# Hymba decoder step: product with v by a difference of blocks, softmax division on ScalarE, last weights split once, the second sample task later

## The chip, the cores and the metric

The program runs on one core of one Trainium2 chip. The metric is the device time of one execution in microseconds (us); the median of three runs of the kernel before is 1681.65 us (1681.14 to 1681.77). One of its executions was also profiled. PE is TensorE (PEld its weight loads), DVE is VectorE, ACT is ScalarE, POOL is GpSimd, SP is SyncE, which issues all transfers here.

## The reference

One layer of a decoder with two heads side by side, in fp32, for 512 prompt tokens and 8 x 8 sampled tokens (576 columns, T) at width 2048:

```python
h = rmsnorm(x, norm_pre); u = h @ w_in          # 2048 x 9760, split into q k v g_a z xbc dt
o_a = swa_prompt(q, k, v, sink)                 # window 128, blocks of 128: each block sees itself and the one before
# sampled tokens: swa_step against a cache of 128 keys
attn_out = rmsnorm(o_a * silu(g_a), attn_norm)
xs, B, C = silu(causal_conv(xbc)); y, h_new = ssd(xs, dt, A, B, C, h0, 128)
ssm_out = grouped_rmsnorm((y + D * xs) * silu(z), ssm_norm)
out = concat(attn_out, ssm_out) @ w_out         # 4096 x 2048
return x + rmsnorm(out, norm_post), new k, v, conv and ssm states
```

## The kernel before

Features lie on partitions, tokens on columns, in two halves p of 288 columns (H). Each weight block (128 x 128) is split in two fp32r parts, high (a ScalarE cast, L332) and low (a VectorE subtraction, L335); so is each block of activations (XU). A product of one weight block with one half is three matmuls of 288 columns, mm3 (L351 to L353). 3352 of them are the bulk of the program: first the columns of w_in (blocks of B, C, x, z, then k, v, and 16 pairs q, g for the attention), then w_out in two passes over the ssm half (pass 0) and the attention half (pass 1). Most blocks from the attention on are computed in pairs, by seven products in place of eight; those use sums of weights made on GpSimd (L269).

Each weight unit of 128 x 512 is loaded into one of nine tiles `raw`, split into one of four tiles `w` (`split_next`, three units ahead of PE), and its `raw` is then free for a later load.

All else is written as Python generators. A scheduler counts a tick for each mm3; `yield n` lets n ticks of mm3 be issued before the generator goes on. The order of instructions on every engine is thereby fixed when the program is built; on the chip each engine works through its own order and waits on semaphores. A generator that goes on later in ticks stands later in every engine's order and in SP's queue.

Names that the change and the prediction touch:

- `rms_x` sums the squares of x (VectorE adds, L564), reduces them on PE (L463) and spreads 1/rms as tile R (L497, copy L613), with which every output of w_in is multiplied (L446, L1206).
- `dt_task` makes the step sizes and decays of the ssm heads: a chain of small VectorE operations (L752 to L773) on a bias loaded from `dtb`, then small matmuls (L782 on).
- Per group g of 8 ssm heads: `scan_task` for four chunks and, as c = 4, the sampled tokens (`sample`, eight `seq` per group: ScalarE L1373, matmul L1378, VectorE L1381); then `gate_task`, whose `renorm` (L1133) reads each block back from memory (`m_d`), scales it and stores it.
- `qb_task`, two per head pair, 32 in all, is the attention: scores (L955, L956), maximum, exponentials (ScalarE L992), denominator (L995, L996), division (L997), transposes on PE (L1002), masks (L1010, L1012), product with v (L1022).
- `smp_task`, one per group of eight pairs (pr = 0, 1), is the attention of the sampled tokens (scores L1063, L1064; L1070 to L1098). The second one runs where the attention ends and pass 0 begins. `attn_end` waits for it, and then takes the norm over the attention (L463 at 1307 us) and runs `renorm` over 16 blocks, which pass 1 reads.
- `mix_task(h)` loads the normed blocks and splits them (L540, L545) as XU for pass h.
- In the last pass blocks 14 and 15 are computed for half p = 0 and then for p = 1, so that `end_task(0)`, the final norm of the first half, lies beside the matmuls of the second: `inv_rms` (L463), spread (L497), then per block a multiplication by 1/rms (L1650), an addition of the residual x (L1654) and a store. The weights of those two blocks are split anew for each half. `x_task` loads the residual.

Of the kernel before, what the change touches and what calls it, by code (L numbers as in the profile page):

```python
# [9 lines left out]
F32 = mybir.dt.float32  # L10
# [168 lines left out]
def kern(ctx: ExitStack, tc: tile.TileContext, a: dict, o: dict):  # L179
# [121 lines left out]
    for p in range(2):  # L301
        for u in range(8):
            jobs.append([b + u, [], [b + u] if p else []])
# [293 lines left out]
    def rms_x():  # L597
# [6 lines left out]
        yield 8  # L604
# [126 lines left out]
    def dt_task():  # L731
# [3 lines left out]
        yield 32  # L735
# [158 lines left out]
    def v_task(st, vn):  # L894
# [10 lines left out]
        S.copy(st.vt[:, :512], pa)  # L905
        V.tensor_copy(vts[:TS, st.pr], pb[:TS, :P])
# [31 lines left out]
    def qb_task(st, jj, m, u):  # L938
# [58 lines left out]
        V.tensor_tensor(p4, p4, den.unsqueeze(2).broadcast_to([P, 4, P]), ALU.mult)  # L997
        tiny.put(t1, t2)
        yield 11
# [8 lines left out]
        for w, tr in enumerate((stri, tri)):  # L1008
            if f and w == 0:
                V.tensor_tensor(pT4[0][:, :, 1], ptv[:, :, 1], tr.unsqueeze(1).broadcast_to([P, 2, P]), ALU.mult)  # L1010
            else:
                V.tensor_tensor(pT[w][:, :512].rearrange("p (e k) -> p e k", e=4), pt.rearrange("p (e k) -> p e k", e=4),  # L1012
                                tr.unsqueeze(1).broadcast_to([P, 4, P]), ALU.mult)
        banks.put(pt)
        yield 9
        for q in range(2):
            qb = 2 * m + q
            w0 = 0 if qb else 1
            for w in range(w0, 2):
                for hf in range(2):  # L1020
                    kc = 128 * (qb - 1 + w) + 64 * hf
                    PE.matmul(u.po[64 * hf:64 * hf + 64, 128 * qb:128 * qb + 128], st.vt[:, kc:kc + 64], pT4[w][:, hf, q],  # L1022
                              start=w == w0, stop=w == 1)
# [3 lines left out]
    def o_task(st, jj, u):  # L1027
# [8 lines left out]
        if st.npv == 8:  # L1036
            smalls.put(st.vt)
# [6 lines left out]
    def smp_task(st):  # L1044
# [9 lines left out]
        yield from wait(lambda: len(st.q) == 8 and st.kready and st.vready)  # L1054
        osb = yield from banks.get()
# [278 lines left out]
    def sample(grp, n, cs, C, Bt, xes, sms, E):  # L1334
# [34 lines left out]
        def seq(b, h0):  # L1369
# [6 lines left out]
            yield 10  # L1376
# [12 lines left out]
        for w in range(2):  # L1389
# [9 lines left out]
            for b, h0 in enumerate(hs, 4 * w):  # L1399
                sch.spawn(seq(b, h0))  # L1400
                yield 5
# [168 lines left out]
    split_in = [0]  # L1570

# [4 lines left out]
    def out_pass(h, evac):  # L1576
        sch.spawn(sums_task(h))
        for kind, *cs in OUT[h]:
# [11 lines left out]
            if h and cs[-1] == 7:  # L1590
                sch.spawn(x_task(0))
# [7 lines left out]
    RO = R  # L1599
# [32 lines left out]
    def end_task(p):  # L1632
# [8 lines left out]
        r = RO[:, t0:t0 + H]  # L1641
        S.copy(r, pa[:, :H])
        engine = [G if (q * NPOOL) % KB < NPOOL else V for q in range(KB)]
        for e0 in range(0, KB, 2):
# [3 lines left out]
            for c in (e0, e0 + 1):  # L1648
                v = part[c][:, t0:t0 + H]
                engine[c].tensor_tensor(v, v, r if engine[c] is G or e0 > 4 else pa[:, :H], ALU.mult)  # L1650
            if e0 == 4:
                banks.put(pa)
            for c in (e0, e0 + 1):
# [126 lines left out]
```

## Time and profile before

| what | value |
|---|---|
| median of three runs | 1681.65 us |
| profiled execution, its own time | 1680.61 us |
| its span, first to last instruction | 1678.8 us |
| mean granted TensorE clock | 0.981 |
| busy: PE / PEld | 1602.4 us (95%) / 1539.9 us (92%) |
| busy: DVE / ACT / POOL | 1141.9 (68%) / 718.8 (43%) / 393.6 us (23%) |
| instructions: PE / DVE / ACT / POOL | 12158 / 2247 / 1699 / 428 |

PE is busy nearly all the time, so time can only come from what PE does, from the stretches in which it waits, and from the two ends of the program. The granted clock stands at half (1.2 in place of 2.4 GHz) in a few short stretches; its mean over a stretch is the column PEclk of the table of stretches.

### The profile page before, as it was taken

The page shows a single profiled execution, that of the slowest core. Times are in us where ns is not written, and L with a number is a line of the kernel's source. Part 1 is how long each engine was busy: PE and PEld are TensorE (multiplying, and loading weights), DVE is VectorE, ACT ScalarE, POOL GpSimd, SP SyncE. Part 2 cuts the span into 40 slices and gives each one's busy share as a digit, 9 for nine tenths or more (in the row PEclk, how much of TensorE's full clock was granted, in tenths as well). Part 3 has the DMA queues.
Part 4 walks back from the last instruction along what each step waited for, and adds up shares of the span by engine and source line. Part 5 has one row for each costly group of instructions (what it writes and reads, how often), then busy time and mean ns, then how long its engine had stood idle before and what let it go on. Part 6 is the DMA issues. An engine that isn't in the chain of part 4 may idle for free.

```text
span 1678.8 us, 31783 instructions
## 1 busy us (share of the span) xinstructions
PE 1602.4 (95%) x12158; PEld 1539.9 (92%) x12158; DVE 1141.9 (68%) x2247; ACT 718.8 (43%) x1699; POOL 393.6 (23%) x428
## 2 busy tenths in 40 slices
PE   8989999999989998999999999999889999999993
PEld 8989999899989997999999999999879999999993
DVE  7656755675568556578898878888775454655557
ACT  6434434444444444444444434444544322544441
POOL 3001223112313222313222122232102211023315
PEclk9989999999999999999999999999999999999996
DMA  6334356656465547652223223233532665623333
GB/s 234 81 79 108 92 182 182 148 161 185 145 144 183 157 127 269 199 120 79 93 76 120 71 83 98 63 100 96 173 111 76 159 201 161 223 77 125 101 116 113
DMA packets 157976, 222.97 MB, mean 133 GB/s; under 512 B 32160, under 2 KB 66080, under 8 KB 157792
## 3 DMA queue, kind: packets, MB, share of 16 engines
q1 hardware_dynamic: 157824, 220.95, 44.3%
q8 instruction: 95, 1.56, 0.4%
q14 instruction: 57, 0.47, 0.1%
HBM read 182.26 MB, written 40.60 MB: 133 GB/s over the span
## 4 chain that ended last, share of the span: by engine, by line
PE 64%; DMA 9%; DVE 6%; issue 2%; ACT 1%; SPq 1%; POOL 0%; DVEq 0%; ACTq 0%
PE bank L351 19%; PE bank L353 18%; PE bank L352 18%; DMA s<-m_d 5%; DMA r_d<-t 2%; PE bank L1022 2%; DVE s L1133 1%; DVE w L335 1%; PE bank L1002 1%; PE bank L955 1%; PE bank L956 1%; DVE s L1650 1%; PE bank L1282 1%; DVE x L545 1%; PE bank L1292 1%
## 5 line engine op out<-in xcount | busy, mean ns | idle before, releaser
L351 PE MATMUL bank<-x,w 128*128 128x288 f32 x3352 | 1017.2, 303 | 6.2 <-DVE eT L423 4.1
L353 PE MATMUL bank<-x,w 128*128 128x288 f32 x3352 | 1000.6, 299 | 15.9 <-DVE w L335 15.7
L352 PE MATMUL bank<-x,w 128*128 128x288 f32 x3352 | 997.5, 298 | 2.0 <-DVE x L545 2.0
L351 PEld LDWEIGHTS bank<-x,w 128*128 128x128 f32 x3352 | 635.2, 189 | 26.6 <-issue 18.6
L353 PEld LDWEIGHTS bank<-x,w 128*128 128x128 f32 x3352 | 636.0, 190 | 20.6 <-DVE w L335 20.6
L352 PEld LDWEIGHTS bank<-x,w 128*128 128x128 f32 x3352 | 635.5, 190 | 8.0 <-issue 4.1
L335 DVE TENSOR_TENSOR w<-raw,w 128x512 fp32r<-128x512 f32 x492 | 396.8, 811 | 164.2 <-ACT w L332 155.8
L332 ACT CAST w<-raw 128x512 fp32r<-128x512 f32 x492 | 299.3, 615 | 348.0 <-PE bank L352 259.5
L269 POOL TENSOR_TENSOR raw<-raw,raw 128x512 f32<-128x512 f32 x52 | 77.1, 1483 | 188.4 <-issue 171.5
L269 POOL TENSOR_TENSOR raw<-sum,raw 128x512 f32<-128x512 f32 x26 | 33.5, 1288 | 187.9 <-DVE w L335 187.9
L1162 DVE SCALAR_TENSOR_TENSOR u<-u,c_convwb,u 128x600 f32<-128x600 f32 x72 | 63.9, 892 | 16.1 <-ACT u L1159 15.0
L992 ACT ACTIVATE m<-m,t 128x128 f32<-128x128 f32 x128 | 49.9, 391 | 33.0 <-DVE t L987 33.0
L1232 ACT ACTIVATE m<-m,a_tok 128x128 f32<-128x128 f32 (+1 forms) x160 | 52.8, 381 | 19.6 <-DMA m<-aT_d 19.6
L833 POOL TENSOR_TENSOR s<-s,s 128x512 f32<-128x512 f32 (+2 forms) x42 | 43.8, 1042 | 67.7 <-ACT s L831 66.8
L545 DVE TENSOR_TENSOR x<-s,x 128x288 fp32r<-128x288 f32 x112 | 49.1, 484 | 15.5 <-ACT x L540 15.4
L1612 POOL TENSOR_TENSOR s<-s,s 128x288 f32<-128x288 f32 x28 | 22.8, 820 | 151.4 <-ACT s L1609 151.4
L269 POOL TENSOR_TENSOR sum<-raw,raw 128x512 f32<-128x512 f32 x26 | 36.0, 1386 | 93.1 <-DMA raw<-in_win_dram 52.0
L1375 POOL TENSOR_TENSOR m<-m,dch 128x512 f32<-128x512 f32 x32 | 37.8, 1210 | 79.3 <-PE bank L1397 60.3
L1268 POOL TENSOR_TENSOR m<-m,de 128x512 f32<-128x512 f32 (+1 forms) x20 | 27.0, 1348 | 109.0 <-DVE m L1261 87.6
L1430 POOL TENSOR_TENSOR s<-s,s 128x576 f32<-128x576 f32 x16 | 24.1, 1503 | 115.4 <-DMA s<-z_d 102.5
L540 ACT CAST x<-s 128x288 fp32r<-128x288 f32 x112 | 42.5, 429 | 18.1 <-DVE s L642 12.4
L831 ACT ACTIVATE s<-s 128x512 f32<-128x512 f32 (+1 forms) x27 | 17.7, 656 | 72.2 <-POOL s L1430 44.6
(248 smaller groups left out, 1671.3 us busy)
## 6 DMA issues: line engine op xcount, KB each, us to landing
raw<-in_win_dram SPq DMA_DIRECT2D x304, 256.0 KB
raw<-in_wout_dram SPq DMA_DIRECT2D x128, 256.0 KB
s<-m_d SPq DMA_DIRECT2D x80, 288.0 KB
m_d<-s SPq DMA_DIRECT2D x48, 288.0 KB
s<-in_xT_dram SPq DMA_DIRECT2D x40, 288.0 KB
m<-aT_d SPq DMA_DIRECT2D x32, 256.0 KB
m<-in_h0T_dram SPq DMA_DIRECT2D x32, 256.0 KB
out_ss_dram<-m SPq DMA_DIRECT2D x32, 256.0 KB
```

What stands on the lines that cost most here:

```text
L269: G.tensor_tensor(dst, x, y, op)
L332: S.copy(w[:, 0], x)
L335: V.tensor_tensor(w[:, 1], x, w[:, 0].bitcast(F32), ALU.subtract)
L351: PE.matmul(out, w[:, 0, c], x[:, 0], start=start, stop=False, skip_group_check=True)
L352: PE.matmul(out, w[:, 0, c], x[:, 1], start=False, stop=False, skip_group_check=True)
L353: PE.matmul(out, w[:, 1, c], x[:, 0], start=False, stop=stop, skip_group_check=True)
L540: S.copy(t[:, 0], src)
L545: V.tensor_tensor(t[:, 1], src, t[:, 0].bitcast(F32), ALU.subtract)
L833: G.tensor_tensor(self.acc[:, c0:c0 + n], self.acc[:, c0:c0 + n], sq[:, :n], ALU.add)
L992: S.activation(p4[:, e], p4[:, e], AF.Exp, bias=nm[:, e:e + 1], scale=0.125, accum_out=den[:, e:e + 1])
L1162: V.scalar_tensor_tensor(y[:, :600], U[:, w:w + 600], cw[:, k, w:w + 1], y[:, :600], op0=ALU.mult, op1=ALU.add)
L1232: S.activation(Mv[q][:n, h, :n], Mv[q][:n, h, :n], AF.Relu, bias=a_tok[:n, c, k:k + 1], scale=-1.0)
```

## The change

- **Product with v.** With P the softmax after its transposition, and masks stri (key later than query in the block before) and tri (not later), the product was (stri P) v_before + (tri P) v_own. Since stri + tri = 1, it is (stri P)(v_before - v_own) + P v_own: `v_task` makes the difference once per group (`st.vd`), and the second mask's multiplication on VectorE (L1012 with tri) becomes a copy on ScalarE.
- **Division.** One VectorE multiplication of 128 x 512 by 1/den becomes four ScalarE activations of 128 x 128 with a scale per partition.
- **Last two blocks.** Their eight weight units leave the list of jobs; `last_units` splits them once into 16 kept tiles. `x_task(0)` starts after that, `x_task(1)` after the first half.
- **end_task.** All 16 multiplications are on VectorE and read 1/rms from the bank; the 16 additions alternate by pairs of blocks between GpSimd and VectorE, two pairs behind. The copy to R goes.
- **Ticks.** rms_x 8 to 14, dt_task 32 to 46, seq 10 to 13 with 7 in place of 5 between them, smp_task of pr = 1 waits 75 more.

```diff
@@ -298,9 +298,6 @@
     nunit[0] += 8
-    for p in range(2):
-        for u in range(8):
-            jobs.append([b + u, [], [b + u] if p else []])
@@ -601,7 +598,7 @@
         slots.put(*xr[1:])
-        yield 8
+        yield 14
         r = yield from inv_rms([xr[0]], D)
@@ -732,7 +729,7 @@
         V.tensor_tensor(dtr[:64, :T], dtr[:64, :T], R[:64], ALU.mult)
-        yield 32
+        yield 46
         An = dtb[:, 32:64]
@@ -903,6 +900,8 @@
         S.copy(st.vt[:, :512], pa)
+        st.vd = yield from smalls.get()
+        V.tensor_tensor(st.vd[:, P:512], st.vt[:, 0:512 - P], st.vt[:, P:512], ALU.subtract)
         V.tensor_copy(vts[:TS, st.pr], pb[:TS, :P])
@@ -994,9 +993,11 @@
         V.reciprocal(den, den)
-        V.tensor_tensor(p4, p4, den.unsqueeze(2).broadcast_to([P, 4, P]), ALU.mult)
+        yield 2
+        for e in range(4):
+            S.activation(p4[:, e], p4[:, e], AF.Copy, scale=den[:, e:e + 1])
         tiny.put(t1, t2)
-        yield 11
+        yield 10
         pt = yield from banks.get()
@@ -1005,12 +1006,13 @@
         pT4 = [t[:, :512].rearrange("p (f q k) -> p f q k", f=2, q=2) for t in pT]
-        for w, tr in enumerate((stri, tri)):
-            if f and w == 0:
-                V.tensor_tensor(pT4[0][:, :, 1], ptv[:, :, 1], tr.unsqueeze(1).broadcast_to([P, 2, P]), ALU.mult)
-            else:
-                V.tensor_tensor(pT[w][:, :512].rearrange("p (e k) -> p e k", e=4), pt.rearrange("p (e k) -> p e k", e=4),
-                                tr.unsqueeze(1).broadcast_to([P, 4, P]), ALU.mult)
+        S.copy(pT[1][:, :512], pt)
+        if f:
+            V.tensor_tensor(pT4[0][:, :, 1], ptv[:, :, 1], stri.unsqueeze(1).broadcast_to([P, 2, P]), ALU.mult)
+        else:
+            V.tensor_tensor(pT[0][:, :512].rearrange("p (e k) -> p e k", e=4), pt.rearrange("p (e k) -> p e k", e=4),
+                            stri.unsqueeze(1).broadcast_to([P, 4, P]), ALU.mult)
         banks.put(pt)
@@ -1018,8 +1020,8 @@
                 for hf in range(2):
-                    kc = 128 * (qb - 1 + w) + 64 * hf
-                    PE.matmul(u.po[64 * hf:64 * hf + 64, 128 * qb:128 * qb + 128], st.vt[:, kc:kc + 64], pT4[w][:, hf, q],
+                    kc = 128 * qb + 64 * hf
+                    PE.matmul(u.po[64 * hf:64 * hf + 64, 128 * qb:128 * qb + 128], (st.vd, st.vt)[w][:, kc:kc + 64], pT4[w][:, hf, q],
                               start=w == w0, stop=w == 1)
@@ -1034,7 +1036,7 @@
         if st.npv == 8:
-            smalls.put(st.vt)
+            smalls.put(st.vt, st.vd)
         yield 2
@@ -1052,6 +1054,8 @@
         yield from wait(lambda: len(st.q) == 8 and st.kready and st.vready)
+        if pr:
+            yield 75
         osb = yield from banks.get()
@@ -1373,7 +1377,7 @@
             G.tensor_tensor(hv, hv, dch[:, 4 + b, h8].unsqueeze(2).broadcast_to([P, 8, 64]), ALU.mult)
-            yield 10
+            yield 13
             pS = yield from banks.get()
@@ -1398,7 +1402,7 @@
                 sch.spawn(seq(b, h0))
-                yield 5
+                yield 7
@@ -1568,6 +1572,21 @@
     split_in = [0]
+    kept = []
+    def last_units():
+        yield from wait(lambda: split[0] == len(jobs))
+        for u in range(8):
+            yield from wait(lambda: loaded[0] > b + u)
+            h, l = yield from smalls.two(r=True)
+            S.copy(h, raw_unit(b + u))
+            yield 1
+            V.tensor_tensor(l, raw_unit(b + u), h.bitcast(F32), ALU.subtract)
+            kept.append((h, l))
+            yield 2
+        sch.spawn(x_task(0))
@@ -1587,8 +1606,9 @@
                 single(*[evac(c) for c in cs], kbs=OUT_ORDER, last=cs[-1] == KB - 1)
-            if h and cs[-1] == 7:
-                sch.spawn(x_task(0))
+            if h and cs[-1] == 11:
+                smalls.borrow = 0
+                sch.spawn(last_units())
@@ -1596,7 +1616,6 @@
     accO, sqO = slots.take(), slots.take()
-    RO = R
     post = [0, 0]
@@ -1638,34 +1657,44 @@
         yield 1
-        r = RO[:, t0:t0 + H]
-        S.copy(r, pa[:, :H])
-        engine = [G if (q * NPOOL) % KB < NPOOL else V for q in range(KB)]
+        later_ = []
         for e0 in range(0, KB, 2):
...
                 v = part[c][:, t0:t0 + H]
-                engine[c].tensor_tensor(v, v, r if engine[c] is G or e0 > 4 else pa[:, :H], ALU.mult)
-            if e0 == 4:
-                banks.put(pa)
-            for c in (e0, e0 + 1):
-                engine[c].tensor_tensor(xv[:, c - e0], part[c][:, t0:t0 + H], xv[:, c - e0], ALU.add)
-            dma(o["yT"][:, e0:e0 + 2, t0:t0 + H], xv)
-            if p == 0:
-                yield 2
-            slots.put(x)
+                V.tensor_tensor(v, v, pa[:, :H], ALU.mult)
+            e = G if e0 % 4 == 0 else V
+            later_.append((e, e0, x, xv))
+            while len(later_) > 2 or e0 == KB - 2 and later_:
+                e, c0, x, xv = later_.pop(0)
+                for c in (c0, c0 + 1):
+                    e.tensor_tensor(xv[:, c - c0], part[c][:, t0:t0 + H], xv[:, c - c0], ALU.add)
+                dma(o["yT"][:, c0:c0 + 2, t0:t0 + H], xv)
+                if p == 0:
+                    yield 2
+                slots.put(x)
+        banks.put(pa)
     out_pass(1, evac_out)
-    sch.spawn(x_task(1))
     for p in range(2):
...
             for u in range(4):
-                steps([(pt, (OUT_ORDER[4 * u + k], p), k, (u, k) == (0, 0), (u, k) == (3, 3)) for k in range(4)])
+                sch.until(lambda: len(kept) > 4 * (c - KB + 2) + u)
+                h, l = kept[4 * (c - KB + 2) + u]
+                for k in range(4):
+                    sch.tick()
+                    w, x = slice(P * k, P * k + P), XU[OUT_ORDER[4 * u + k], p]
+                    PE.matmul(pt[:, :H], h[:, w], x[:, 0], start=(u, k) == (0, 0), stop=False, skip_group_check=True)
+                    PE.matmul(pt[:, :H], h[:, w], x[:, 1], start=False, stop=False, skip_group_check=True)
+                    PE.matmul(pt[:, :H], l[:, w], x[:, 0], start=False, stop=(u, k) == (3, 3), skip_group_check=True)
             evac_out(c)(p, pt[:, :H], None)
             banks.done(pt)
+        if p == 0:
+            drop(*[(kb, 0) for kb in range(KB)])
+            sch.spawn(x_task(1))
         sch.spawn(end_task(p), 1)
```

What moves shows in the orders of the two programs. First the instructions of PE where pass 0 begins (L351 to L353 are mm3, L1063 and L1064 the scores of the second sample task), before:

```order
L351 MATMUL bank_70<-x_12991,w_96 128x288
L352 MATMUL bank_70<-x_12991,w_96 128x288
L353 MATMUL bank_70<-x_12991,w_96 128x288
L1063 MATMUL bank_65<-m_12634,m_10311 64x128
L1064 MATMUL bank_65<-s_9888,m_10311 64x64
L1063 MATMUL bank_65<-m_12634,m_10311 64x128
L1064 MATMUL bank_65<-s_9888,m_10311 64x64
L351 MATMUL bank_68<-x_12999,w_96 128x288
```

and the same place of the change, where those three lines are L348 to L350:

```order
L348 MATMUL bank_72<-x_13084,w_96 128x288
L349 MATMUL bank_72<-x_13084,w_96 128x288
L350 MATMUL bank_72<-x_13084,w_96 128x288
L348 MATMUL bank_70<-x_13091,w_96 128x288
L349 MATMUL bank_70<-x_13091,w_96 128x288
```

The sample task's matmuls are gone from there; its first ones now stand 73 mm3 later.

Next ScalarE in the attention, one head pair (L974 copies scores, L992 exponentials, L332 casts of weights), before:

```order
L332 CAST w_97<-raw_87 128x512
L332 CAST w_98<-raw_90 128x512
L974 COPY m_9738<-bank_69 128x256
L974 COPY m_9738<-bank_72 128x256
L332 CAST w_95<-raw_91 128x512
L992 ACTIVATE m_9738,t_79<-m_9738,t_78 128x128 x4
L993 ACTIVATE t_79<-t_79 128x4
L332 CAST w_96<-raw_92 128x512
```

and in the change (L998 is the division, L1010 the copy that takes the place of the tri mask):

```order
L329 CAST w_97<-raw_91 128x512
L329 CAST w_98<-raw_85 128x512
L973 COPY m_8451<-bank_71 128x256
L973 COPY m_8451<-bank_68 128x256
L998 ACTIVATE m_8375<-m_8375,t_73 128x128 x4
L329 CAST w_95<-raw_86 128x512
L991 ACTIVATE m_8451,t_75<-m_8451,t_74 128x128 x4
L992 ACTIVATE t_75<-t_75 128x4
L329 CAST w_96<-raw_87 128x512
L1010 COPY m_8522<-bank_66 128x512
```

The division of the first half of a head pair now stands behind the copies of the second half's scores and ahead of one cast of weights, which PE needs.

Last VectorE in end_task(0), beside the matmuls of the second half (L1650 multiplication, L1654 addition, L335 weights, L1620 evacuation), before:

```order
L1650 TENSOR_TENSOR s_12958<-s_12958,bank_68 128x288
L1654 TENSOR_TENSOR s_16520<-s_12958,s_16520 128x288
L335 TENSOR_TENSOR w_98<-raw_91,w_98 128x512
L1650 TENSOR_TENSOR s_13587<-s_13587,bank_68 128x288
L1654 TENSOR_TENSOR s_16522<-s_13587,s_16522 128x288
L1650 TENSOR_TENSOR s_13935<-s_13935,bank_68 128x288
L1650 TENSOR_TENSOR s_13936<-s_13936,bank_68 128x288
L1654 TENSOR_TENSOR s_16524<-s_13935,s_16524 128x288
L1654 TENSOR_TENSOR s_16524<-s_13936,s_16524 128x288
L335 TENSOR_TENSOR w_95<-raw_92,w_95 128x512
L1620 TENSOR_TENSOR s_15146<-s_15146,bank_67 128x288
```

and in the change (L1667 multiplication, L1673 addition, L1639 evacuation):

```order
L1667 TENSOR_TENSOR s_14248<-s_14248,bank_66 128x288
L1667 TENSOR_TENSOR s_14249<-s_14249,bank_66 128x288
L1673 TENSOR_TENSOR s_17368<-s_13570,s_17368 128x288
L1673 TENSOR_TENSOR s_17368<-s_13741,s_17368 128x288
L1667 TENSOR_TENSOR s_14509<-s_14509,bank_66 128x288
L1667 TENSOR_TENSOR s_14510<-s_14510,bank_66 128x288
L1639 TENSOR_TENSOR s_15246<-s_15246,bank_68 128x288
L1667 TENSOR_TENSOR s_14755<-s_14755,bank_66 128x288
```

No split of weights stands between them any more; the evacuation of block 15 stands behind all 24 operations.

## Rows read from the trace of the kernel before

**Rows 1.** Busy time of each engine in stretches of the whole program.

```profile
core 0: us, PE busy (x) PEld busy (x) DVE busy (x) ACT busy (x) POOL busy (x), PEclk, DMA share, GB/s
45.00:111.00 66.00, 58.94 (x395) 55.67 (x394) 39.41 (x93) 23.70 (x45) 3.85 (x22) 0.90 0.34 86
280.00:750.00 470.00, 449.40 (x3381) 425.64 (x3379) 294.59 (x558) 204.79 (x440) 114.33 (x129) 0.99 0.60 169
750.00:1200.00 450.00, 449.66 (x3599) 434.50 (x3598) 378.30 (x771) 209.43 (x592) 116.52 (x107) 1.00 0.29 89
1200.00:1250.00 50.00, 38.22 (x273) 34.50 (x272) 38.29 (x115) 24.21 (x82) 1.52 (x2) 0.86 0.49 160
1425.00:1636.00 211.00, 211.00 (x1591) 210.98 (x1589) 122.92 (x214) 96.38 (x205) 48.49 (x47) 1.00 0.40 129
1636.00:1662.00 26.00, 17.12 (x111) 16.12 (x108) 19.36 (x44) 4.79 (x11) 12.34 (x13) 0.82 0.26 91
```

**Rows 2.** Who waited for whom: us in total, times, longest.

```profile
DVE s L1133 <- DMA s<-m_d: 74.0, 29, 7.6
...
PE bank L353 <- DVE w L335: 15.7, 16, 3.3
PE bank L1378 <- ACT r L1373: 7.0, 3, 3.2
PE bank L1063 <- DVE m L979: 4.4, 1, 4.4
PE bank L782 <- DVE s L773: 4.3, 1, 4.3
PE bank L463 <- DVE s L564: 2.2, 1, 2.2
```

**Rows 3.** VectorE in order of time, 60 to 90 us: start, length.

```profile
61.17 0.75 DVE L734 TENSOR_TENSOR s<-s,R 64x576 f32<-64x576 f32 x1 [3.94 <-ACT R L613]
```

**Rows 4.** Groups by form of VectorE and ScalarE: busy us, mean ns, idle before.

```profile
L997 DVE TENSOR_TENSOR m<-m,t 128x512 f32<-128x512 f32 x32 | 22.1, 692 | 1.1
L1012 DVE TENSOR_TENSOR m<-bank,c_tri 128x512 f32<-128x512 f32 x32 | 21.8, 681 | 0.0
...
L992 ACT ACTIVATE m<-m,t 128x128 f32<-128x128 f32 x128 | 49.9, 391 | 33.0 <-DVE t L987 33.0
```

**Rows 5.** VectorE, then PE in order of time: one half of a head pair.

```profile
827.37 0.69 DVE L997 TENSOR_TENSOR m<-m,t 128x512 f32<-128x512 f32 x1
...
831.62 0.60 PE L1002 MATMUL bank<-ident,m 128*128 128x128 f32 x4
```

**Rows 6.** VectorE in order of time: last block of attention renorm, first splits for pass 1.

```profile
1391.31 0.82 DVE L1133 SCALAR_TENSOR_TENSOR s<-s,c_ganorm,s 128x576 f32<-128x576 f32 x1 [2.53 <-DMA s<-m_d]
...
1428.59 1.56 DVE L545 TENSOR_TENSOR x<-s,x 128x288 fp32r<-128x288 f32 x4
```

**Rows 7.** Groups by form of VectorE, and one of GpSimd, in end_task.

```profile
L1654 DVE TENSOR_TENSOR s<-s,s 128x288 f32<-128x288 f32 x20 | 13.7, 703 | 0.4
...
L1650 DVE TENSOR_TENSOR s<-s,R 128x288 f32<-128x288 f32 x12 | 9.6, 816 | 0.0
...
L1650 DVE TENSOR_TENSOR s<-s,bank 128x288 f32<-128x288 f32 x8 | 3.4, 445 | 3.4 <-ACT R L1642 3.4
...
L1654 POOL TENSOR_TENSOR s<-s,s 128x288 f32<-128x288 f32 x12 | 11.3, 942 | 0.9
```

**Rows 8.** VectorE and PE in order of time, the end of the program.

```profile
1639.46 0.46 DVE L1650 TENSOR_TENSOR s<-s,bank 128x288 f32<-128x288 f32 x1 [1.44 <-ACT R L1642]
...
1651.95 0.40 PE L353 MATMUL bank<-x,w 128*128 128x288 f32 x1 [3.28 <-DVE w L335]
...
1655.63 0.45 DVE L1620 TENSOR_TENSOR s<-s,bank 128x288 f32<-128x288 f32 x1
...
1662.07 0.46 DVE L1650 TENSOR_TENSOR s<-s,bank 128x288 f32<-128x288 f32 x1 [1.97 <-ACT R L1642]
...
1675.11 0.46 DVE L1654 TENSOR_TENSOR s<-s,s 128x288 f32<-128x288 f32 x1
```

## Prediction

> **What bounds the kernel now.** I first read the busy time by engine. PE stands at 95%, VectorE at 68%, ScalarE at 43%. The change leaves the number of mm3 as it is and takes no matmul from PE, so a gain can only come out of the stretches in which PE waits. The second view is busy time by stretches [rows 1]. In the attention (750 to 1200 us) PE is idle for 450.00 - 449.66 = 0.34 us, and in the last pass (1425 to 1636) not at all; 1591 matmuls in 211.00 us there make 0.40 us for one mm3, which is my tick. PE's idle time lies in four other places: the start (45 to 111, 7.1 us idle), the ssm scans (280 to 750, 20.6 us), the handover from the attention to pass 0 (1200 to 1250, 11.8 us, with a granted clock of 0.86), and the tail (1636 to 1662, 8.9 us). Third, the list of waits says who is late there [rows 2]: splits of weights (L335, 15.7 us in all, many of them around the handover and the tail), the scaled input of the sampled tokens' state (L1373, 7.0 us), the bank that the last block of the attention frees (copied out by L979) for the second sample task's scores (L1063, 4.4 us), the dt chain (L773, 4.3 us) and the sum of squares (L564, 2.2 us). Last, the chain that ended last is PE, except at the end, where VectorE's final norm is on it. So I price the edits place by place, not by the engine time they save.
>
> **Start.** L463 of rms_x now stands 6 mm3 later, so its 2.2 us wait goes [rows 2]. But R cannot come sooner: VectorE's chain behind it begins at 61.17 after 3.94 us of waiting for the copy of R [rows 3], and what PE does in the meantime it would have done later. I expect the next split of weights to wait for part of it. dt_task stands 14 ticks, 5.6 us, later for PE, more than its 4.3 us wait [rows 2]; but convolution steps on VectorE come ahead of the chain in that time, and so the chain is later too. Best, both waits go: -6.5. Worst, they re-sort and add one: +1. I take **-2**.
>
> **Scans.** seq waits 13 ticks in place of 10 before L1378 and starts every 7 in place of 5. Three more ticks are 1.2 us against waits of 7.0/3 = 2.3 us on average, 3.2 at the longest [rows 2], so the distance alone covers half. The sampled tokens of each group also move, by 17 to 85 mm3 in the four groups, and other work then meets them. What stays is VectorE's wait for the blocks that renorm reads back, 74.0 us in 29 waits, the longest 7.6 us [rows 2]: any chain behind such a wait is late wherever it stands. Best, the 7.0 go and 3 more of the 20.6 idle: -10; worst, a new wait like one of these: +2. I take **-4**.
>
> **Attention.** VectorE loses 32 divisions of 0.692 and 32 masks of 0.681 us, 43.9 us in all [rows 4]. ScalarE gains 128 activations; L992, of the same shape and engine, takes 0.391 [rows 4], so 50.0 us, and 32 copies of a bank. ScalarE is busy for 209.43 of 450 us [rows 1] and has the room. PE waits for neither today, so 43.9 us off VectorE are worth nothing here. The two differences for `st.vd` are nothing beside that. What hides the division is the distance to the transposes: in one half of a head pair it ended at 827.37 + 0.69 = 828.06, and the first transpose began at 831.62, 3.56 us later [rows 5]. Now the division stands two ticks (0.8 us) later and lasts 4 x 0.391 = 1.56 us, while the transposes stand one tick (0.4 us) later: 3.56 - 0.8 - 0.87 + 0.4 = 2.3 us are left for the copies and casts ahead of it on ScalarE. I take **0**; a gain is bounded by the 0.34 us of idle time, a loss, if a few of the 32 are late, by +5.
>
> **Handover.** The second sample task leaves for a place 73 mm3 = 29 us later. Its matmuls are the same work there. Here the 4.4 us wait of L1063 goes [rows 2], since by then the attention's banks are long free. Around it PE is idle for 7.4 us more, and a mean clock of 0.86 says that 0.28 of the 50 us, 14 us, ran at the lower level (1.2 GHz); at a busy share of 38.22/50 = 0.76 [rows 1], matmuls cost 14 x 0.76/2 = 5.3 us more there than at 2.4 GHz. Everything together is 17.1 us. But the splits for pass 0 on VectorE, busy for 38.29 of the 50 us [rows 1], stay, and the waits for them with it. Bounds: -4 (the one wait) to -14. I take half of the 17.1, **-8.5**, since sample work and splits share VectorE here.
>
> **Norm over the attention.** It moves with the sample task by 29 us. The last renorm block begins on VectorE at 1391.31 and would begin at about 1420; the splits of pass 1 begin at 1428.59 [rows 6]. So some 8 us are left, and PE has mm3 of pass 0 to do. Value **0**, from -2 to +3.
>
> **Tail.** Before, eight units were split again beside end_task(0): VectorE did splits between its multiplications, and the last wait of PE for one was 3.28 us, at 1651.95 [rows 8]. These go. VectorE takes on all 16 multiplications, from the bank, at 0.445, and 8 additions at 0.703 [rows 7]: 7.1 + 5.6 = 12.7 us. It begins without the 0.40 us copy to R, at 1639.46 - 0.4 = 1639.1, so the evacuation of block 15, which the order puts behind all of it, begins at 1651.8 in place of 1655.63 [rows 8]: -3.8. PE, with its splits ready, will have ended its matmuls some microseconds earlier and wait for VectorE. The second end_task ran from 1662.07 to 1675.11 + 0.46 = 1675.57 [rows 8], 13.5 us; with 12.7 and no copy, -1.2. Additions can cost 0.46 (the last one, GpSimd done [rows 8]) to 0.94 (GpSimd's own price [rows 7]); with these bounds each half is 10.8 to 14.6, and the evacuation's lead shrinks or grows by 2. Value **-5.0**, from -1 to -9. The rows show why the bank matters: the multiplication costs 0.816 with R in SBUF, 0.445 with the bank, both beside GpSimd [rows 7].
>
> The Trainium skill has a rule for that (page "SBUF — State Buffer", section "Who interferes with whom"): a VectorE instruction with two SBUF inputs and a GpSimd instruction that reads SBUF exclude each other, one with a single SBUF input does not. The two prices of the multiplication agree. By it GpSimd's 8 additions (7.5 us at the row's 0.942) would run beside the 7.1 us of multiplications, VectorE's 8 then alone at 0.46, and each half would be 10.8 us: the tail -8.8 in place of -5.0.
>
> **Sum:** -2 - 4 + 0 - 8.5 + 0 - 5.0 = -19.5. The profiled execution's own time is 1680.61, 1.0 below the median of the runs: 1680.6 - 19.5 + 1.0 = **1662**.
>
> **Rivals.**
> *The middle gives nothing back.* For it: VectorE's waits for memory [rows 2] do not shorten, and at the handover the splits themselves may be the limit, so waits only change their name. Against it: the sample task has its own wait there. Then only L1063's 4.4 and the tail's 5.0 remain, with nothing from start and scans: 1681.65 - 9.4 = 1672.
> *The division becomes the bound* (slower). ScalarE works in order, and the division stands behind the second half's score copies and ahead of a cast that PE needs. Against it: 2.3 us of cover, as worked out above. For it: 3.56 us was one of 32, and a ScalarE waiting for those copies' matmuls holds the division too. It decides where the transposes wait 19.5/32 = 0.6 us each on average: from there on the kernel is not faster. At 1 us each: 1662 + 32 = 1694.
> *Pass 1 waits for the later norm.* For it: only some 8 us are left [rows 6], and renorm waits for memory up to 7.6 us at a time [rows 2]. Against it: 16 blocks need not all be there at the first mm3. If it slips by 18, 10 beyond the 8, the time is 1672.
>
> **Chances.** My forecast 0.70, the empty middle 0.18, pass 1 late 0.06, the division as bound 0.06. The division's case is not always dear enough to be slower: about 0.04 slower, 0.02 the same; 2 more in 100 that the other losses just cancel the gains. A measurement of this kernel tells some 0.2%, 3.4 us, from no change. So faster 0.92, same 0.04, slower 0.04. The ends of the terms differ from the values taken by +3/-4.5, +6/-6, +5/0, +4.5/-5.5, +3/-2, +4/-4; as independent errors these make +11/-10. The upper end goes to 1674, so that it holds the empty middle, the lower to 1648.
>
> **What would show it.** Right: no wait of PE for the sum of squares near 50 us; the dt wait at 2 to 3 us or gone; no waits at L1378 of 2 to 3 us; from 1200 to 1250 no wait for the sample task's scores and a clock nearer 1; the attention still with almost no idle PE, its transposes waiting for nothing on ScalarE; no waits for L335 in the last 25 us, but a wait of PE of 3 to 4 us before the last sum of squares; VectorE's two end_tasks 11 to 13 us each. Wrong: transposes in the attention waiting for the division; matmuls of pass 1 waiting for splits (L545's) around 1430 us; or the same total idle time between 280 and 1250 under other names.

## The result and the profile after

The changed kernel takes 1654.84 us (median of 4 runs, 1651.62 to 1660.33) against 1681.71 us for the kernel before; the ratio is 0.9842, 95% interval [0.9814, 0.987]. The profiled execution has a span of 1652.0 us against 1678.8, 26.8 us less. The forecast was 1662, and the range held the time. The gain is 27 us where 19.5 had been worked out, and part of it lies elsewhere than the sum put it.

The same stretches of the kernel after as in [rows 1], with the same columns. The kernel after is ahead of the kernel before: by 15 us where the attention begins, by 9 at the handover, by 18 where the tail begins and by 27 at its end. So a stretch with the same times does not hold quite the same work. The handover's work stands in 1191 to 1241 here (the last row but one), and the tail is shown 26 us earlier:

```profile
45.00:111.00 66.00, 61.30 (x415) 58.81 (x414) 43.35 (x99) 25.00 (x46) 8.84 (x22) 0.90 0.36 90
...
280.00:750.00 470.00, 459.31 (x3481) 438.84 (x3480) 307.26 (x579) 214.97 (x462) 115.77 (x132) 0.99 0.58 163
750.00:1200.00 450.00, 442.21 (x3516) 426.86 (x3515) 341.69 (x708) 257.43 (x731) 114.15 (x105) 0.99 0.33 99
1200.00:1250.00 50.00, 48.15 (x370) 46.25 (x370) 41.66 (x115) 31.95 (x97) 6.02 (x3) 0.96 0.55 177
...
1191.00:1241.00 50.00, 44.27 (x330) 42.26 (x328) 43.05 (x99) 34.10 (x99) 7.70 (x5) 0.93 0.60 195
...
1610.00:1636.00 26.00, 21.76 (x168) 21.45 (x167) 14.47 (x47) 3.91 (x10) 8.05 (x10) 0.96 0.62 205
```

PE's idle time in the scans went from 20.6 to 10.7 us, at the handover from 11.8 to 5.7 (1.9 between 1200 and 1250 us, but two of its waits now come earlier). Between 750 and 1200 us there were 0.34 us, and there are now 7.8. Of these, 3.9 are those two waits, for the first splits of pass 0. They ended behind 1200 us before and end ahead of it now (PE in order of time, first the kernel before, then the kernel after):

```profile
1204.39 0.40 PE L351 MATMUL bank<-x,w 128*128 128x288 f32 x1 [1.70 <-ACT x L540]
...
1206.55 0.61 PE L352 MATMUL bank<-x,w 128*128 128x288 f32 x1 [1.76 <-DVE x L545]
```

```profile
1195.55 0.40 PE L348 MATMUL bank<-x,w 128*128 128x288 f32 x1 [2.13 <-ACT x L537]
...
1197.71 0.61 PE L349 MATMUL bank<-x,w 128*128 128x288 f32 x1 [1.75 <-DVE x L542]
```

The new loss in the attention is one wait of 3.7 us at 764. VectorE's busy time in these 450 us fell from 378.30 to 341.69 us, as it should, and ScalarE's rose from 209.43 to 257.43.

The list of waits after, PE's own rows (engine, line, for whom: us in total, times, longest). L332 is the L335 of before, L1382 is L1378, L779 is L782, L460 is L463:

```profile
PE bank L350 <- DVE w L332: 17.2, 8, 3.9
PE bank L460 <- ACT s L1628: 2.7, 1, 2.7
...
PE bank L1024 <- ACT m L1010: 1.8, 1, 1.8
...
PE bank L779 <- DVE s L770: 1.0, 1, 1.0
...
PE bank L1003 <- ACT m L998: 0.3, 1, 0.3
```

Against [rows 2], the waits at L1378, for the sample task's scores and for the sum of squares are gone, and the dt wait went from 4.3 to 1.0. The splits cost as much as before (17.2 and 15.7), but in 8 waits in place of 16: fewer and longer. Three of them stand alone, near 469, 635 and 761 us. The new attention leaves two traces on PE. One is 0.3 us for a late division. The other is 1.8 us at 1222 us, in the handover, where the last product with v (L1024) waits for the copy that took the place of the tri mask (L1010). With the attention as before, in the run of that name below, PE waits there 1.3 us for a mask on VectorE, so about half a microsecond of it is the new attention's.

**Where the 26.8 us went.** PE's order of mm3 is the same in both kernels, so I read for mm3 number k the start of its last matmul in either trace, and took differences over stretches of k. The same was done for the twelve kernels of the experiments, each with one profiled execution, so most stretches were measured many times:

| stretch (mm3) | before | after | difference | all traces, without the edit that acts there | all traces, with it |
|---|---|---|---|---|---|
| start (0 to 300) | 165.06 | 161.82 | -3.2 | 165.1 to 167.2 (3) | 159.8 to 163.8 (11) |
| scans (300 to 1472) | 583.74 | 571.47 | -12.3 | 583.7 to 588.8 (4) | 570.5 to 575.1 (7) |
| first units of the attention (1500 to 1560) | 28.93 | 35.41 | +6.5 | 28.9 (4) | 35.0 to 36.0 (7) |
| rest of the attention (1560 to 2350) | 393.79 | 393.11 | -0.7 | 393.5 to 394.1 (3) | 393.1 to 393.8 (11) |
| handover, norm (2350 to 2900) | 272.75 | 263.95 | -8.8 | 271.8 to 272.8 (3) | 264.0 to 267.4 (11) |
| last pass (2900 to 3320) | 167.70 | 167.71 | 0.0 | | 167.6 to 167.8 (14) |
| tail (from 3320) | 45.24 | 36.47 | -8.8 | 45.2 (3) | 36.4 to 37.1 (10) |

(Before mm3 0 the kernel after is 0.5 us later, and 1472 to 1500 is equal. The number of matmuls and of their columns is the same in both kernels in every row. The counts differ since some kernels change other things in a stretch: the three with 24 ticks in renorm are left out of the scans and of the first units, and the run with R in SBUF out of the tail. The edit that acts on both middle rows is that of seq's ticks, as the experiments show.) Within each row the two groups lie apart, but for the rest of the attention, where they overlap.

### The profile page after: what moved, and what is told of

Its sections match the earlier page's. It is cut to its first block, busy times and chain, and to the rows that moved or that the text cites. A ratio compares the mean times of both kernels' runs of the same rounds, so it can differ in the third digit from the quotient of the medians.

```text
span 1652.0 us, 31869 instructions
## 1 busy us (share of the span) xinstructions
PE 1598.8 (97%) x12158; PEld 1542.6 (93%) x12158; DVE 1095.8 (66%) x2185; ACT 771.1 (47%) x1849; POOL 389.4 (24%) x420
## 3 DMA queue, kind: packets, MB, share of 16 engines
q1 hardware_dynamic: 157824, 220.95, 44.5%
## 4 chain that ended last, share of the span: by engine, by line
PE 80%; DVE 8%; DMA 6%; ACT 2%; issue 2%; SPq 1%; POOL 0%; DVEq 0%; ACTq 0%; POOLq 0%
PE bank L348 23%; PE bank L350 23%; PE bank L349 22%; DMA s<-m_d 4%; PE bank L1024 2%; DVE w L332 1%; DMA r_d<-t 1%; DVE u L1166 1%; PE bank L1286 1%; PE bank L1003 1%; DMA s<-z_d 1%; PE bank L954 1%; PE bank L955 1%; PE bank L1298 1%; DVE s L1667 1%
## 5 line engine op out<-in xcount | busy, mean ns | idle before, releaser
L348 PE MATMUL bank<-x,w 128*128 128x288 f32 x3288 | 999.9, 304 | 6.4 <-DVE eT L420 2.6
L350 PE MATMUL bank<-x,w 128*128 128x288 f32 x3288 | 983.4, 299 | 17.2 <-DVE w L332 17.2
L349 PE MATMUL bank<-x,w 128*128 128x288 f32 x3288 | 980.6, 298 | 1.8 <-DVE x L542 1.8
L348 PEld LDWEIGHTS bank<-x,w 128*128 128x128 f32 x3288 | 625.7, 190 | 26.5 <-issue 15.1
L350 PEld LDWEIGHTS bank<-x,w 128*128 128x128 f32 x3288 | 626.8, 191 | 19.2 <-DVE w L332 19.2
L349 PEld LDWEIGHTS bank<-x,w 128*128 128x128 f32 x3288 | 625.8, 190 | 7.2 <-issue 3.8
L332 DVE TENSOR_TENSOR w<-raw,w 128x512 fp32r<-128x512 f32 x476 | 386.7, 818 | 130.4 <-ACT w L329 120.5
L329 ACT CAST w<-raw 128x512 fp32r<-128x512 f32 x476 | 289.4, 615 | 270.5 <-PE bank L349 226.0
L1166 DVE SCALAR_TENSOR_TENSOR u<-u,c_convwb,u 128x600 f32<-128x600 f32 x72 | 67.4, 940 | 24.0 <-ACT u L1163 22.9
L991 ACT ACTIVATE m<-m,t 128x128 f32<-128x128 f32 x128 | 49.9, 391 | 38.7 <-DVE t L986 38.7
L998 ACT ACTIVATE m<-m,t 128x128 f32<-128x128 f32 x128 | 41.0, 392 | 45.5 <-DVE t L995 45.4
L1163 ACT ACTIVATE u<-u,c_convwb 128x600 f32<-128x600 f32 x24 | 21.2, 889 | 65.5 <-DVE u L443 61.7
```

Source lines behind the costliest of these rows:

```text
L329: S.copy(w[:, 0], x)
L332: V.tensor_tensor(w[:, 1], x, w[:, 0].bitcast(F32), ALU.subtract)
L348: PE.matmul(out, w[:, 0, c], x[:, 0], start=start, stop=False, skip_group_check=True)
L349: PE.matmul(out, w[:, 0, c], x[:, 1], start=False, stop=False, skip_group_check=True)
L350: PE.matmul(out, w[:, 1, c], x[:, 0], start=False, stop=stop, skip_group_check=True)
L991: S.activation(p4[:, e], p4[:, e], AF.Exp, bias=nm[:, e:e + 1], scale=0.125, accum_out=den[:, e:e + 1])
```

## The experiments

The kernel before had medians of 1681.7 to 1688.7 us on the chips that were used. So each run is given as its ratio to the kernel before on the same chip, and its trace against those of the other runs.

**The changed kernel again** (no edit).

> The changed kernel once more, unedited, as the measure of its spread: four runs lay between 1651.6 and 1660.3 us. If the spread comes from VectorE's waits for the blocks that renorm reads back from memory, the waits of PE for a split (L332) of 3 to 4 us near 469, 637 and 761 us come again with other lengths, and the time lies between 1650 and 1661. If they were an accident of one execution, they are gone and the time is near 1648.

1657.87 us, ratio 0.9819 [0.9805, 0.9832]. PE's waits near 469, 635 and 761 us came again at 471, 637 and 760, with 3.8, 2.9 and 4.5 us. They belong to the kernel and not to one execution. They don't account for the spread: the two traces differ most in the handover with the norm (267.4 us against 264.0).

**The second sample task 75 ticks earlier.**

```diff
-        if pr:
-            yield 75
```

> Second sample task 75 ticks earlier, as before; all else changed. Theory (the sample task's scores and the splits for pass 0 meet at the handover): the waits for L1067 come back near 1210 and the clock there falls to about 0.86; 8 to 10 us slower than the changed kernel, 1663 to 1665. Rival (the lighter VectorE of the new attention was what freed the handover): 0 to 3 us slower, 1655 to 1658.

1665.11 us, ratio 0.9861 [0.9847, 0.9874], 7 us slower than the changed kernel on this chip. The waits of PE from 1180 to 1440 us:

```profile
PE bank L1065 <- DVE m L978: 4.2, 1, 4.2
PE bank L350 <- DVE w L332: 3.4, 6, 1.2
...
PE bank L1065 <- ACT x L537: 2.6, 1, 2.6
```

The sample task's scores (here L1065) wait as they did before [rows 2]. The handover with the norm takes 272.2 us, as in the two other kernels with the early task. That the attention's VectorE was lighter did not help it. The theory holds; over all traces the 75 ticks are worth 6.6 us, the difference of the means of that row (272.3 and 265.7).

**seq with its old ticks, and with one of the two.**

```diff
-            yield 13
+            yield 10
...
-                yield 7
+                yield 5
```

> seq with 10 and 5 ticks as before; all else changed. Theory (the three more ticks cover L1377 and its neighbours): the waits of L1382 for ScalarE come back with 5 to 8 us in all between 280 and 750 us, time 1660 to 1663. Rival (the scans gained because the shift by rms_x and dt_task moved every group against the rest): within 2 us of the changed kernel, 1653 to 1657.

1664.07 us, ratio 0.9848 [0.9823, 0.9872]. The second kernel has 13 and 5:

```diff
-                yield 7
+                yield 5
```

> seq with 13 ticks before L1382 as in the changed kernel, but 5 between the eight, as before; all else changed. Theory (the three more ticks cover the waits): the waits for L1377 stay away, within 2 us of the changed kernel, 0.981 to 0.985. Rival (the wider spacing does it, since the eight hold VectorE and ScalarE too densely): as with both undone, waits at L1382 near 650 us or splits late beside it, 0.985 to 0.988.

1666.85 us, ratio 0.9864 [0.984, 0.9889]. PE's waits from 280 to 780 us, first with both old:

```profile
PE bank L350 <- DVE w L332: 10.1, 9, 2.9
PE bank L1382 <- ACT r L1377: 6.7, 3, 3.2
PE bank L1286 <- DVE m L1279: 4.6, 3, 1.9
```

then with 13 and 5:

```profile
PE bank L1286 <- DVE m L1279: 6.1, 4, 2.7
PE bank L350 <- DVE w L332: 5.4, 3, 2.9
PE bank L1413 <- ACT m L1408: 4.1, 1, 4.1
PE bank L1003 <- ACT m L998: 2.0, 1, 2.0
```

This is the most telling pair. Thirteen ticks took every wait at L1382 away, as I had argued, and with the old spacing they won nothing clear: the scans take 586.3 us against 587.6, since other waits stand in their place. With 13 ticks in place, the spacing of 7 wins 13.6 us (586.3 against 572.7, the mean of the seven kernels that have it), and the theory written for the second run falls. The same spacing loses 6.5 us at the entry of the attention: with 5 ticks those first units take 28.9 us, with 7 they take 35. The eight sampled tokens spread over 16 more ticks make the later steps of each group later, and the fourth group's renorm then stands inside the attention: its first block (L1137) comes on VectorE behind mm3 1447 with 13 and 5, behind mm3 1512 with 13 and 7. So seq's ticks are worth some 6 to 7 us in all, 12.3 to 13.6 less 6.5. The gain does not come from that renorm's leaving the scans: at mm3 1400, ahead of its place in either kernel, the kernel with 13 and 5 has already lost 13.0 us to the changed one since mm3 300, and 10.8 of them fall between mm3 1250 and 1300. Which of the other steps the gain hangs on stays open, and 10 with 7 was not tried.

**The attention as before, and the new attention alone.** The first is the changed kernel with these parts undone, and with them the difference of blocks:

```diff
-        for e in range(4):
-            S.activation(p4[:, e], p4[:, e], AF.Copy, scale=den[:, e:e + 1])
+        V.tensor_tensor(p4, p4, den.unsqueeze(2).broadcast_to([P, 4, P]), ALU.mult)
...
-        S.copy(pT[1][:, :512], pt)
+        for w, tr in enumerate((stri, tri)):
```

> Attention as before: division and both masks on VectorE, product with v by blocks; all else changed. Theory of the prediction (PE waited for neither): within 2 us of the changed kernel, 1653 to 1657, and PE as busy as before between 780 and 1190 us. Rival (VectorE, 44 us lighter, gives the handover and the late renorm of the last group their time): 4 to 9 us slower, 1659 to 1664, with the lost time at 760 to 775 or at 1195 to 1250 us.

1654.38 us, ratio 0.9797 [0.9783, 0.9811]. The second is the kernel before with the same parts put in.

> The kernel before with the new attention alone (division and second mask on ScalarE, difference of blocks). Theory of the prediction: 0, ratio 0.999 to 1.001. If the division on ScalarE is late for the transposes: PE waits for L998 in the attention, 1.002 or more. If the lighter VectorE frees the handover: fewer waits between 1195 and 1250 us, 0.995 to 0.998.

1685.78 us, ratio 0.9983 [0.997, 0.9996]. By the medians the new attention costs 3.5 us in one kernel and gives 3.0 in the other. In the attention the traces show neither: from mm3 1560 on it takes 393.1 to 393.8 us with the new, 393.5 to 394.1 with the old, and PE's only wait from 770 to 1190 us in the kernel with it alone is

```profile
PE bank L1091 <- DVE t L1076: 0.3, 1, 0.3
```

for the sampled tokens, none for the division. The edit that took some 40 us off VectorE (busy for 1135.6 us with the old attention, 1095.8 in the changed kernel) is worth between nothing and 0.7 us in its own stretch. The rest of what the medians show I can't place.

**rms_x and dt_task with their old ticks.**

```diff
-        yield 14
+        yield 8
...
-        yield 46
+        yield 32
```

> rms_x with 8 and dt_task with 32 ticks as before; all else changed. Theory (the start is worth 2.75 us by itself and the rest of the program does not hang on it): the waits for the sum of squares near 50 us and for the dt chain near 85 us come back, 2 to 4 us slower than the changed kernel's ratio of 0.982 to 0.984, so 0.984 to 0.986. Rival (the shift of the scans' groups against renorm is what won the scans): the waits between 280 and 750 us grow as well, 6 us or more slower, 0.987 and over.

1660.83 us, ratio 0.9853 [0.9828, 0.9878]. The waits from 45 to 111 us are back:

```profile
PE bank L779 <- DVE s L770: 4.4, 1, 4.4
PE bank L460 <- DVE s L561: 2.2, 1, 2.2
PE bank L350 <- DVE w L332: 0.6, 1, 0.6
```

In the changed kernel the same stretch has 1.0, none and 2.2, and one more of 1.5 for a cast (L329): 2.5 us less in all. The scans are as in the changed kernel (573.7). The theory holds.

**The last two blocks and end_task as before** (all parts of the change on `jobs`, `last_units`, `kept` and `end_task` undone).

> The last two blocks and end_task as before; all else changed. Theory: the tail's 8.7 us come back and nothing else moves, ratio 0.987 to 0.990. Rival (the loads and tiles that the kept units take cost something in the last pass, and the tail won more than it shows): less than 5 us slower, 0.985 to 0.987.

1665.81 us, ratio 0.9874 [0.9851, 0.9897]. The tail takes 45.2 us, as in the kernel before, and no other stretch moves. Theory held.

**1/rms from SBUF in end_task.**

```diff
+        r = R[:, t0:t0 + H]
+        S.copy(r, pa[:, :H])
...
-                V.tensor_tensor(v, v, pa[:, :H], ALU.mult)
+                V.tensor_tensor(v, v, r, ALU.mult)
```

> In end_task the 16 multiplications read 1/rms from a copy in SBUF (R) in place of the bank; all else changed. By the exclusion of VectorE's two SBUF inputs and GpSimd's reads: a multiplication beside GpSimd's additions costs 0.8 us in place of 0.38, alone about 0.46; some 6 of 16 run beside them per half, so each half is 4 to 7 us longer with the copy, the kernel 7 to 13 us slower, ratio 0.987 to 0.991. If reading SBUF in place of the bank is all: 0.08 us each, 1.3 us and the copy's 0.4 per half, 3 us slower, 0.984 to 0.986. If GpSimd is the one that waits: VectorE's multiplications stay under 0.5 and GpSimd's additions grow past 1.2.

1667.07 us, ratio 0.9874 [0.9851, 0.9897]; the tail takes 44.5 us, 8 more than with the bank. VectorE in the second end_task of the changed kernel, in order of time (start, length, xcount in a row), and the GpSimd additions beside its first row:

```profile
1637.45 3.00 DVE L1667 TENSOR_TENSOR s<-s,bank 128x288 f32<-128x288 f32 x8 [1.54 <-PE bank L494]
1640.38 1.34 DVE L1673 TENSOR_TENSOR s<-s,s 128x288 f32<-128x288 f32 x2
1641.64 1.53 DVE L1667 TENSOR_TENSOR s<-s,bank 128x288 f32<-128x288 f32 x4
1643.10 1.35 DVE L1673 TENSOR_TENSOR s<-s,s 128x288 f32<-128x288 f32 x2
1644.37 1.53 DVE L1667 TENSOR_TENSOR s<-s,bank 128x288 f32<-128x288 f32 x4
1645.83 2.03 DVE L1673 TENSOR_TENSOR s<-s,s 128x288 f32<-128x288 f32 x4
...
1637.99 3.05 POOL L1673 TENSOR_TENSOR s<-s,s 128x288 f32<-128x288 f32 x4 [7.27 <-DVE s L1667]
```

and with R, VectorE's and then GpSimd's rows:

```profile
1647.87 5.42 DVE L1669 TENSOR_TENSOR s<-s,R 128x288 f32<-128x288 f32 x8 [1.97 <-ACT R L1661]
...
1656.62 0.81 DVE L1675 TENSOR_TENSOR s<-s,s 128x288 f32<-128x288 f32 x2
...
1648.47 1.85 POOL L1675 TENSOR_TENSOR s<-s,s 128x288 f32<-128x288 f32 x2 [8.73 <-issue]
1651.13 1.85 POOL L1675 TENSOR_TENSOR s<-s,s 128x288 f32<-128x288 f32 x2 [0.82 <-issue]
1654.53 1.85 POOL L1675 TENSOR_TENSOR s<-s,s 128x288 f32<-128x288 f32 x2 [1.55 <-issue]
1657.88 1.90 POOL L1675 TENSOR_TENSOR s<-s,s 128x288 f32<-128x288 f32 x2 [1.50 <-DVE s L1669]
```

Eight multiplications from the bank take 3.00 us, 0.375 each, though four additions of GpSimd run beside them. From SBUF they take 5.42, beside four such additions as well. Reading SBUF alone is not dear: at 1656.62, between two bursts of GpSimd (the third ends at 1656.38, the fourth begins at 1657.88), two additions with both inputs in SBUF take 0.81 us, 0.405 each. So 5.42 - 8 x 0.405 = 2.2 us were lost beside 3.7 us of GpSimd's additions. The Trainium skill (page "SBUF — State Buffer", section "Who interferes with whom") has the two exclude each other. The trace agrees as to which instructions meet, and shows some 60% of GpSimd's time lost to VectorE and not all of it; two additions of GpSimd also take 1.85 us here, where four took 3.05 beside the bank's multiplications. The theory of the exclusion expected 7 to 13 us, and the tail lost 8.

**More ticks in renorm.** In all ssm groups, then only in the second and fourth, then the same with the old attention:

```diff
-        yield 10
+        yield 24 if row else 10
```

> In the renorm of the four ssm groups 24 ticks in place of 10 between the factors' load and the first block; all else changed. Theory (VectorE stands 7.5 us before its first multiplication of each renorm because the factors and the first block arrive late, and PE runs out of splits there): the waits of PE for L332 near 470, 637 and 760 us go, with the half clock behind the last, 8 to 13 us faster, ratio 0.974 to 0.979. Rival (the splits are late because their own loads stand behind the factors' load in SP's queue): the same waits of PE stay under L329 or the load, no change, 0.982 to 0.984.

1654.75 us, ratio 0.9807 [0.9782, 0.9832].

```diff
-        yield 10
+        yield 24 if row in (2, 4) else 10
```

> 24 ticks in place of 10 ahead of renorm's first block, now only for the second and the fourth ssm group, where that took PE's wait away (near 470 and 760 us), and not for the third, where it made another. Theory: 4 us less by 500 us and 5 us less around 770 us than the changed kernel, none of the 6.4 us near 650; ratio 0.975 to 0.979. Rival (a wait that goes there always comes back later in the scans): 0.980 and over.

1648.94 us, ratio 0.9769 [0.9753, 0.9785].

> The same, with the attention as before (division and masks on VectorE, product with v by blocks). If the new attention costs the 3.5 us that the medians of the two kernels showed, this is 3 us faster than the run with the new attention, ratio 0.973 to 0.977. If it is worth nothing, as their traces showed, the two are within 2 us of one another.

1650.95 us, ratio 0.9779 [0.9759, 0.9798]. The edit was made for this place of the changed kernel, VectorE in order of time:

```profile
753.49 0.18 DVE L995 RECIPROCAL t<-t 128x4 f32<-128x4 f32 x1
761.18 0.82 DVE L1137 SCALAR_TENSOR_TENSOR s<-s,c_gssm,s 128x576 f32<-128x576 f32 x1 [7.51 <-DMA s<-m_d]
...
763.71 0.68 DVE L332 TENSOR_TENSOR w<-raw,w 128x512 fp32r<-128x512 f32 x1
```

Then the chain that ended last through it (start, length, what):

```profile
744.94 9.94 DMA r_d<-t
...
754.95 0.33 SPq L845
755.28 0.05 issue
755.33 5.74 DMA s<-m_d
...
761.18 0.82 DVE s L1137
```

and PE:

```profile
764.45 0.61 PE L350 MATMUL bank<-x,w 128*128 128x288 f32 x1 [3.69 <-DVE w L332]
```

The store of the norm's factors goes out as two transfers, of 2.0 and 0.2 KB. From the issue of the second to its landing it took 9.94 us, their load was issued at 754.95, and the first block's load behind it (288 KB) took 5.74. The order has the multiplication of renorm 18 ticks (7 us) after the factors' load; VectorE came to it at 753.67 and stood for 7.5 us, and the split that PE needed stood behind it. PE waited 3.69 us, and then ran at the lower level of its clock (1.2 GHz, 0.50 in the second row):

```profile
760.00:765.00 5.00, 1.31 (x8) 1.07 (x7) 3.72 (x9) 1.37 (x7) 0.82 (x1) 0.84 0.61 206
765.00:770.00 5.00, 5.00 (x22) 4.75 (x20) 3.51 (x6) 1.88 (x6) 1.27 (x1) 0.50 0.83 296
770.00:775.00 5.00, 5.00 (x44) 4.81 (x44) 3.13 (x7) 3.51 (x8) 0.25 (x2) 0.98 0.31 92
```

22 matmuls begin in 5 us in place of 44. So the loss of 6.5 us is 3.7 of waiting and the rest clock. With 14 more ticks in all groups the first units of the attention take 30.4 us in place of 35.4, but the third group's renorm gave PE a new wait of 6.4 us at 651, which the theory had not foreseen, and the ratio of 0.981 missed both ranges. Without the third group that wait isn't there, and the kernel is faster than both: its ratio is 0.005 to 0.007 below the two of the changed kernel, each taken against the kernel before on its own chip. The old attention adds nothing to it (2 us slower in the medians, 1.5 us faster in the traces), which is what no effect looks like.

## Why the prediction was right, and where its sizes were off

- **Scans, -4 in the sum, -12.3 measured (with the entry of the attention -5.8).** This is the term that was mis-sized. I priced the three more ticks before L1382 by the 7.0 us of waits there, and took the spacing of 7 for a detail. The runs show the reverse: without those waits nothing is won, and with the spacing 12 to 14 us are. It lies beyond the -10 that I took as the best case. PE's idle time fell by 9.9 us; the granted clock from 280 to 750 us is 0.99 in both kernels, so the clock does not account for the other 2.4, and what does was not found.
- **Attention, 0, measured -0.7 in its body and +6.5 at its entry.** The -0.7 is no clear effect, as the groups of that row overlap. The step on the division held for this kernel: transposes wait for L998 0.3 us in all. It is not safe in general, since in the kernel with 13 and 5 ticks one of them waited 2.0 us. What failed is the step that looked at the scans and the attention apart. I had written that the sampled tokens move by up to 85 mm3 and that any chain behind a wait of renorm is late wherever it stands, but not that the fourth group's renorm would then stand ahead of splits in the attention, where PE has no slack at all. The +5 of the bound was given for late divisions, and the loss came from elsewhere.
- **Handover, -8.5, measured -8.8 with the norm** in this execution, and -6.6 over the means of all traces. Right in place: the scores' two waits, 4.4 and 2.7 us, went, and over the same work the clock rose from 0.86 to 0.93. That the size fits is in part luck, for I had taken half of all that could be lost there without working out which half. The two waits of the first splits of pass 0, 2.1 and 1.8 us, stay, and the 1.8 us for L1010 are new.
- **Norm over the attention, 0.** It is in the same row of the table. PE was idle for 5.2 of the 110 us from 1315 to 1425 us after and for 5.8 before, and the last pass took 167.6 to 167.8 us in every kernel: pass 1 did not wait. The last block of renorm began at 1404.99 and the first splits of pass 1 at 1412.57, 7.6 us later, near the 8 that I had worked out.
- **Tail, -5.0, measured -8.8.** The places were right: no wait for L332 in the last 25 us, a wait of 2.7 us before the last sum of squares (3 to 4 expected), the evacuation of block 15 earlier. The size was off because I multiplied mean durations. The multiplication's mean is 443 ns after as it was 445 before [rows 7], but eight in a row take 3.00 us: one begins before the last has ended. The second end_task took from 1637.45 to 1645.83 + 2.03 = 1647.86, 10.4 us, where 12.7 stood in the sum. By the Trainium skill's rule I had worked out 10.8 and a tail of -8.8, which is what was measured. That agreement is in part luck: the 16 multiplications took 6.1 us in place of 7.1, and VectorE's eight additions 4.7 in place of 3.7, since GpSimd's ran beside some of them.
- **Start, -2, measured -3.2**, and 4.0 between the means of that row's traces (165.9 and 161.8). Both waits went or shrank, and 2.2 us came back as a wait for a split, as expected, with 1.5 more for a cast.

The sum came out 7 us short. The scans gave 8.3 us more than forecast and the entry of the attention took 6.5 back, and it is luck that these two nearly cancel; the rest of the difference is the tail's 3.8 and small parts.

Of the rivals, the empty middle, the division as bound and the late pass 1 were all wrong here. The first falls by the table, where scans and handover gain. The second was put to the test by the runs with the old attention; the third only by the last pass's constant time.

## What to carry to other kernels

- Where each engine works through a fixed order, the price of a delay is what the order puts behind it, not the wait that it removes: the 7.0 us of waits were worth nothing at the old spacing, and a spacing that shifts whole chains was worth twelve there and lost 6.5 further on.
- Ask of a chain that is moved later which wait it brings along, and whether the new neighbours have slack. Here a read-back from memory, which had cost PE little in its old place, cost 6.5 us in a stretch that had no idle time.
- Compare two kernels by the same work, not by the same times. The kernel after was 9 us ahead at the handover, and stretches with equal times put 3.9 us of pass 0's waits into the attention.
- Price a row of equal instructions by the time of the whole row, not by the mean duration times the count.

## What was not expected of the hardware

- The same program's executions differ by some microseconds: the changed kernel's spread by 8.7 us (1651.62 to 1660.33) on one chip and by 2.9 on another, the kernel before's by 2.2 on the first and by 5.4 to 10.5 on the three others, and its medians run from 1681.7 to 1688.7 us. What makes it was not found.
- After a wait of 3.7 us PE ran at the lower clock (0.50) from 765 to 770 us, though it was busy all that time. A wait is dearer than its length: 6.5 us for 3.7.
- The store of the norm's factors to memory (r_d, 2.0 and 0.2 KB) took 9.94 us from the second issue to the landing, and the load of one block of 288 KB behind it 5.74. A small transfer is not a short one.
